# One layout for all dense products: weights held in TensorE, 256 tokens moving, and buffers shifted within 512 bytes

## Chip, cores and metric

The kernel runs on one core of a Trainium2 chip. The metric is the device time of one execution in microseconds, as the median of several runs. Before the change it is 2276.02 us (3 runs, 2275.32 to 2277.13).

## What is computed

A trunk of two layers over one sequence of 256 tokens with 2048 channels, in float32. Layer 0 mixes tokens with a diagonal state-space model (S5), layer 1 with a convolution module; a SwiGLU feed-forward network (FFN) with 5632 hidden channels follows each.

```
for i in range(2):
    shift/scale/gate = split(silu(c) @ ada_w[i] + ada_b[i])        # six vectors of 2048
    h = x * (1 + sc_m) + sh_m
    y = s5(h) then vg = y @ w_glu; vg[:, :d] * sigmoid(vg[:, d:])   # layer 0
    y = glu(h @ w_pw1) -> depthwise conv(31) -> norm -> silu -> @ w_pw2   # layer 1
    x = layer_norm(ALPHA * x + (1 + gt_m) * y)
    h = x * (1 + sc_f) + sh_f
    y = (silu(h @ w_g) * (h @ w_v)) @ w_down
    x = layer_norm(ALPHA * x + (1 + gt_f) * y)
```

The dense products are those with w_glu (2048 x 4096), w_pw1 (2048 x 4096), w_pw2 (2048 x 2048), twice the FFN's gate and value weights (2048 x 11264) and twice w_down (5632 x 2048). Together they read most of the 574 MB that come from HBM; the rest is chiefly ada_w.

## The kernel before

The activations lie with channels on the partitions: X and the input h of a product are tiles of 16 chunks of 128 channels with 256 tokens each. Each float32 product is made of three products in the float32r type: with weights split into whi + wlo and tokens into a high and a low part, it is whi x high, whi x low and wlo x high.

**Units.** A dense product is cut into gemms of 512 output columns, and a gemm into units of four chunks of 128 input channels, 1 MB of weights each. For a unit, SyncE issues the load into one of four raw buffers, ScalarE rounds it to whi (L833) and VectorE takes the remainder as wlo (L834); whi and wlo have two buffers each. Then TensorE runs its matmuls: 4 chunks x 3 products. The pool of these weight buffers is opened in `start_dense`, behind a pool `const2` of small constants; the hidden activations f2 of an FFN lie in pools f0 and f1, opened later. Each pool's start follows from what was allocated ahead of it.

**Two forms.** With `wide` (L889) a 128 x 128 block of the tokens is the operand held in TensorE and 512 columns of weights move past it; a bank of PSUM then holds 128 tokens by 512 output channels. One unit is 24 such matmuls. Without `wide` (L893) a 128 x 128 block of the weights is held and the 256 tokens move; a bank holds two blocks of 128 channels by 256 tokens. One unit is 48 such matmuls. Most gemms are wide. Narrow are the last gemm ahead of each layer norm (last of w_glu, last of w_pw1, first and last of w_pw2, last down gemm of each layer). The first gemm behind each norm but one, `panel` (L1005), also holds the weights; its tokens carry two further columns, 258 in all, so a chunk steps by 1032 bytes.

**After a gemm.** In the wide form the sums have tokens on the partitions, so they are turned: `turned` (L905) makes four 128 x 128 transposes into another PSUM bank. For gated products ScalarE (sigmoid) and VectorE (products) first make the gated tile in SBUF, then that tile is turned. For down and w_pw2 gemms, `add_later` (L1100, L1101) copies both banks to SBUF, one on ScalarE and one on VectorE, and turns the copies. What follows reads the turned bank: `split` (L909, L910: high and low part of the FFN's hidden tile), `residual` (L1060: two multiply-adds on VectorE into X for each of two halves), or `conv_in`, ahead of the convolution.

**What sets the order.** Each engine works its queue in program order. A list called `turning` holds what is put off: `turning.put(n, fn)` runs fn n units later, right after that unit's loads, rounding and remainder have been written down and ahead of its matmuls. All turns are put off by two units. The projection of c (`ada`) is spread over the units as well: a rate says how many of its 1 MB steps go with one unit, a load on SyncE's queue and one multiply-add of 2.1 us on VectorE (L701). PSUM has four accumulator banks; a gemm takes two.

Of the kernel before, what the change touches and what calls it, by code (L numbers as in the profile page):

```python
# [19 lines left out]
P = 128  # L20
# [484 lines left out]
def kernel(  # L505
# [335 lines left out]
    def gemm(wsrc, k0, kch, segs, x2, wp, feed=None, ahead=None, banks=((0, 1), (2, 3)), before={}, acc=None, wide=True):  # L841
# [12 lines left out]
        for u, u0 in enumerate(units):  # L854
# [23 lines left out]
            for part in ((0,), (1,)) if last and not in_turn else ((0, 1),):  # L878
# [5 lines left out]
                for n, (wt, k, h) in enumerate(order):  # L884
                    x = x2(u0 + k)[:, h]
                    first, end = u == 0 and n == 0, last and n == len(order) - 1
                    for bank in part:
                        if wide:
                            nc.tensor.matmul(  # L889
                                acc[bank].rearrange("p a b -> p (a b)"), x[:, bank * HALF:(bank + 1) * HALF], wt[:, k], start=first, stop=end)  # L890
                            continue
                        for i, m in enumerate(banks[bank]):
                            nc.tensor.matmul(  # L893
                                acc[bank][:, i], wt[:, k, m * P:(m + 1) * P], x, start=first and i == 0, stop=end and i == 1)
# [3 lines left out]

    def turned(u, c0, then):

        b = aux("turned")
        for k in range(2):
            for t in range(2):
                o = k * SEQ + t * HALF
                nc.tensor.transpose(b[:, o:o + HALF], u[t][:, c0 + k * P:c0 + (k + 1) * P], ident)  # L905
        then(b.rearrange("p (k n) -> p k n", n=SEQ))
# [168 lines left out]
    def gated(wsrc, off, width, sp, then, entry=None, wide=True, **kw):  # L1075
# [11 lines left out]
        acc = gemm(wsrc, 0, NCH, segs, xh, banks=((0, 2), (1, 3)), wide=wide, **kw)  # L1087
# [4 lines left out]
        if wide:  # L1092
            turning.put(2, lambda: turned([t[:, 0], t[:, 1]], 0, then))
        else:
            then(t)

    def add_later(ys, gt, ch, stats, sp):

        yt = [sp.tile([P, 2, SEQ], F32, tag="sg", name="yt", bufs=2).rearrange("p a b -> p (a b)") for _ in range(2)]
        nc.scalar.copy(out=yt[0], in_=ys[0].rearrange("p a b -> p (a b)"))  # L1100
        nc.vector.tensor_copy(out=yt[1], in_=ys[1].rearrange("p a b -> p (a b)"))  # L1101
        for i in range(2):
            turning.put(2, lambda i=i: turned(yt, 256 * i, lambda b: residual(b, gt, ch + 2 * i, stats)))
# [110 lines left out]
    def ffn(layer, gt, stats, wp, sp, fp, entry, ahead=None, output=None, follow=None):  # L1214

        f0, out = 0, None
        for part, nf in enumerate((24, 20)):
            f2 = fp.tile([P, 24, 2, SEQ], F32R, tag="f2", name=f"f2{layer}{part}")
            fh, fl = f2[:, :, 0], f2[:, :, 1]
            for f in range(0, nf, 2):  # L1220
# [14 lines left out]
                acc = gemm(ffn_w_gu[layer], 0, NCH, gu_cols(f0 + f), xh, wp)  # L1235
# [5 lines left out]
                turning.put(2, lambda t=t, h=fh[:, f:f + 2], l=fl[:, f:f + 2]: turned([t[:, 0], t[:, 1]], 0, lambda b: split(b, h, l)))  # L1241
            ada.finish(layer, 5)
            for q in range(4):
# [6 lines left out]
                ys = gemm(ffn_w_down[layer], f0, nf, [(512 * q, 512)], chunks(f2), wp, ahead=ahead if last else None, wide=not last)  # L1250
# [262 lines left out]
    with mctx:  # L1513
# [19 lines left out]
        for i in range(8):  # L1533
            if i == 7:
                fp = f0ctx.enter_context(tc.tile_pool(name="f0", bufs=1, reuse_waits="tile"))
                raw = entry_raw(fp)
                entry = enter("f0", stats, 0, 0, raw, 7)
            with ExitStack() as order:
                if i == 0:
                    order.enter_context(tc.manual_schedule(engines={mybir.EngineType.PE}))  # L1540
                gated(s5_w_glu[0], 256 * i, D, sp, lambda t, i=i: residual(t, mod[0][:, 2], 2 * i, stats), wp=wp, wide=i < 7,
# [152 lines left out]
        for i in range(8):  # L1694
            ada.hold = i > 5
            gated(cv_w_pw1[0], 256 * i, D, sp, lambda t, i=i: conv_in(i, t), entry if i == 0 else None, wp=wp, wide=i < 7,
# [89 lines left out]
```

## Time and profile before

| | |
|---|---|
| median of the runs | 2276.02 us |
| the profiled execution | 2276.45 us |
| its span, first to last instruction | 2274.7 us |
| mean granted TensorE clock | 0.989 |
| DMA, mean over the span | 255 GB/s |
| S5, before the dense products | 0 to some 200 us |
| w_glu | 200 to 404 us |
| FFN of layer 0 | 404 to 1160 us |
| convolution module | 1160 to 1510 us |
| FFN of layer 1 and the output | 1510 to 2275 us |

The page gives busy time by engine (PE is TensorE's matmuls, PEld its weight loads, DVE VectorE, ACT ScalarE, POOL GpSimd, SP SyncE) and the chain of work that ended last. Groups of instructions are written as "line engine operation output<-inputs". In a timeline a row is a run of like instructions: start in us, us to the end of the last one, and xcount. A matmul's recorded duration runs into its successors, so the price of one in a stream is the distance from one row's start to the next one's, divided by the count.

### The profile page before, as it was taken

How to read it: one execution, taken by the hardware profiler on the slowest of the kernel's cores; microseconds unless marked ns; L12 is line 12 of the kernel's file. 1: busy time of each engine (PE TensorE's matmuls, PEld its weight loads, DVE VectorE, ACT ScalarE, POOL GpSimd, SP SyncE). 2: the span in 40 equal slices, each digit the busy share in tenths (PEclk: the TensorE clock that was granted, in tenths of full speed). 3: DMA queues.
4: the chain of work that ended last, by engine and by line, in shares of the span. 5: the costliest groups of instructions: out<-in, count | busy, mean ns of one | idle time of the engine just before them, and what ended most of it. 6: DMA issues, size and time to landing. Idle time of an engine off the chain costs nothing.

```text
span 2274.7 us, 33445 instructions
## 1 busy us (share of the span) xinstructions
PE 2221.7 (98%) x13619; PEld 1804.2 (79%) x13619; DVE 1671.7 (73%) x1826; ACT 1018.8 (45%) x1237; POOL 157.0 (7%) x265
## 2 busy tenths in 40 slices
PE   7999999999999999999999998999999999999998
PEld 4556778987788888787897786898888888888888
DVE  8897898877777777777988788878755444545474
ACT  4775335644343333343455434556433433434343
POOL 5761000000000000000010110000000000000000
PEclk8999999999999999999999999999999999999998
DMA  9998899599999899999857775757865555555542
GB/s 333 342 317 279 296 340 311 173 313 330 323 328 328 322 321 324 317 327 322 309 157 203 225 213 191 255 191 236 281 222 185 186 195 191 186 185 193 192 165 80
DMA packets 380608, 579.48 MB, mean 255 GB/s; under 512 B 13875, under 2 KB 277939, under 8 KB 365987
## 3 DMA queue, kind: packets, MB, share of 16 engines
q1 hardware_dynamic: 379862, 576.82, 74.9%
q8 instruction: 107, 1.75, 0.3%
q0 software_dynamic: 352, 0.45, 0.1%
q14 instruction: 47, 0.39, 0.1%
q10 hardware_dynamic: 240, 0.08, 0.0%
HBM read 573.72 MB, written 3.57 MB: 254 GB/s over the span
## 4 chain that ended last, share of the span: by engine, by line
PE 79%; DVE 10%; DMA 4%; ACT 4%; issue 2%; SPq 0%; POOL 0%; DVEq 0%; ACTq 0%
PE acc L889 65%; PE acc L893 6%; DVE wlo L834 3%; DMA raw<-in_ffn_w_gu_dram 3%; ACT whi L833 2%; PE acc L1005 2%; PE turned L905 2%; PE conv L1677 1%; DVE adaacc L701 1%; PE y L499 1%; DMA raw<-in_s_w_glu_dram 1%; PE ada L629 1%; DMA raw<-in_ada_w_dram 1%; DVE pin L476 1%; PE adar L709 0%
## 5 line engine op out<-in xcount | busy, mean ns | idle before, releaser
L834 DVE TENSOR_TENSOR wlo<-raw,whi 128x2048 fp32r<-128x2048 f32 x344 | 788.8, 2294 | 456.7 <-ACT whi L833 448.6
L833 ACT CAST whi<-raw 128x2048 fp32r<-128x2048 f32 x344 | 655.6, 1906 | 812.1 <-PE acc L889 442.7
L889 PE MATMUL acc<-whi,h 128*128 128x512 f32 x3648 | 893.4, 394 | 7.6 <-ACT whi L833 7.2
L889 PEld LDWEIGHTS acc<-whi,h 128*128 128x128 f32 x3648 | 680.5, 189 | 161.7 <-ACT whi L833 13.1
L889 PE MATMUL acc<-wlo,h 128*128 128x512 f32 x1824 | 461.8, 390 | 0.8 <-DVE wlo L834 0.6
L889 PEld LDWEIGHTS acc<-wlo,h 128*128 128x128 f32 x1824 | 341.5, 188 | 74.3 <-DVE wlo L834 3.8
L889 PE MATMUL acc<-whi,f 128*128 128x512 f32 x1248 | 300.9, 391 | 0.0
L701 DVE SCALAR_TENSOR_TENSOR adaacc<-rawa,c_act,adaacc 128x2048 f32<-128x2048 f32 (+1 forms) x135 | 284.4, 2107 | 0.4
L889 PEld LDWEIGHTS acc<-whi,f 128*128 128x128 f32 x1248 | 232.8, 188 | 49.5 <-ACT whi L833 1.7
L889 PE MATMUL acc<-wlo,f 128*128 128x512 f32 x624 | 156.5, 389 | 0.0
L889 PEld LDWEIGHTS acc<-wlo,f 128*128 128x128 f32 x624 | 117.1, 188 | 24.3
L1607 POOL TENSOR_TENSOR lw<-fold,wtap 128x1024 f32<-128x1024 f32 x12 | 26.3, 2195 | 1055.5 <-PE acc L893 866.2
L629 PE MATMUL ada<-raw,c_rep 128*32 128x512 f32 (+1 forms) x576 | 71.3, 592 | 6.0 <-DMA raw<-in_ada_w_dram 3.6
L1238 ACT ACTIVATE fsg<-acc 128x256 f32<-128x256 f32 x84 | 31.6, 379 | 97.7 <-PE acc L889 97.7
L893 PEld LDWEIGHTS acc<-h,whi 128*128 128x128 f32 x512 | 63.6, 192 | 8.9 <-ACT h L909 4.2
L893 PE MATMUL acc<-h,whi 128*128 128x256 f32 x512 | 67.3, 286 | 3.4 <-ACT h L909 2.2
L1182 POOL CAST lnmh<-lno 128x2 fp32r<-128x2 f32 x1 | 0.2, 182 | 885.9 <-DVE lno L68 885.9
L1239 DVE TENSOR_TENSOR fsg<-acc,fsg 128x256 f32<-128x256 f32 x84 | 35.0, 418 | 17.0 <-ACT fsg L1238 17.0
L1677 PE MATMUL conv<-vs,lw 128*32 128x256 f32 x720 | 42.2, 380 | 0.1
L893 PE MATMUL acc<-f,whi 128*128 128x256 f32 x320 | 40.7, 284 | 0.0
L893 PEld LDWEIGHTS acc<-f,whi 128*128 128x128 f32 x320 | 39.3, 192 | 0.2
L476 DVE TENSOR_TENSOR_SCAN pin<-rho,pin 128x1024 f32<-128x1024 f32 x16 | 36.7, 2294 | 0.5
(349 smaller groups left out, 1839.7 us busy)
## 6 DMA issues: line engine op xcount, KB each, us to landing
raw<-in_ffn_w_gu_dram SPq DMA_DIRECT2D x352, 512.0 KB, 4.7
rawa<-in_ada_w_dram SPq DMA_DIRECT2D x128, 1024.0 KB, 5.5
raw<-in_ffn_w_down_dram SPq DMA_DIRECT2D x88, 1024.0 KB, 5.1
raw<-in_ada_w_dram SPq DMA_DIRECT2D x64, 1024.0 KB, 7.7
raw<-in_s_w_glu_dram SPq DMA_DIRECT2D x64, 512.0 KB, 5.9
raw<-in_cv_w_pw_dram SPq DMA_DIRECT2D x64, 512.0 KB, 6.0
raw<-in_cv_w_pw_dram SPq DMA_DIRECT2D x16, 1024.0 KB, 5.9
vs<-scr SPq DMA_DIRECT2D x40, 142.0 KB, 5.3
```

The costliest lines, as they stand in the source:

```text
L476: done = v.tensor_tensor_scan(out=z, data0=rh.rearrange("p q r c -> p (q r c)"), data1=z, initial=0.0, op0=MUL, op1=ADD)
L629: nc.tensor.matmul(acc[32 * (k % 4):32 * (k % 4) + 32, :], c_rep[:, kk, :], r[:, k, :], start=kk < 4, stop=kk >= NCH - 4)
L701: nc.vector.scalar_tensor_tensor(out=acc, in0=r[:, i], scalar=c_act[:, kk:kk + 1], in1=acc, op0=MUL, op1=ADD)
L833: m1 = nc.scalar.copy(out=self.hi[:, :kn], in_=r[:, :kn])
L834: m2 = nc.vector.tensor_tensor(out=self.lo[:, :kn], in0=r[:, :kn], in1=self.hi[:, :kn].bitcast(F32), op=SUB)
L889: nc.tensor.matmul(acc[bank].rearrange("p a b -> p (a b)"), x[:, bank * HALF:(bank + 1) * HALF], wt[:, k], start=first, stop=end)
L893: nc.tensor.matmul(acc[bank][:, i], wt[:, k, m * P:(m + 1) * P], x, start=first and i == 0, stop=end and i == 1)
L905: nc.tensor.transpose(b[:, o:o + HALF], u[t][:, c0 + k * P:c0 + (k + 1) * P], ident)
L1005: nc.tensor.matmul(acc[m][:, 0:EW], wt[:, k, m * P:(m + 1) * P], xx[:, 4 * u + k], start=u == 0 and n == 0, stop=u == 3 and n == len(order ...
L1238: nc.scalar.activation(out=t[:, i], in_=gv[:, 0], func=AF.Sigmoid)
L1239: nc.vector.tensor_tensor(out=t[:, i], in0=gv[:, 0], in1=t[:, i], op=MUL)
L1677: nc.tensor.matmul(acc[32 * q:32 * q + 32, :], lw[:, q, g, :], vs[:, q, 4 * g:4 * g + SEQ], start=g == 0, stop=g == n - 1)
```

## The change

- The wide form is gone, and with it `turned` and `add_later`. All gemms hold 128 x 128 blocks of weights and move 256 tokens.
- For the gated products of the FFN each accumulator bank holds one block of gate and the matching block of value channels (`banks=((0, 2), (1, 3))`), as those of w_glu and w_pw1 did in the narrow form.
- What follows a gemm reads the accumulators, or the gated tile in SBUF, directly: the FFN's `split` and the residuals one unit later instead of two, `conv_in` two units later as before.
- Three tiles named "room" are allocated and not used: 48 floats (192 bytes of each partition) ahead of the weight buffers and 80 floats (320 bytes) ahead of f2 in each of the pools f0 and f1. By the change's own words the weight buffers then start at 384, and h and f at 448, modulo 512 bytes. h lies ahead of all of it and doesn't move.

```diff
                     for bank in part:
-                        if wide:
-                            nc.tensor.matmul(
-                                acc[bank].rearrange("p a b -> p (a b)"), x[:, bank * HALF:(bank + 1) * HALF], wt[:, k], start=first, stop=end)
-                            continue
                         for i, m in enumerate(banks[bank]):
                             nc.tensor.matmul(
                                 acc[bank][:, i], wt[:, k, m * P:(m + 1) * P], x, start=first and i == 0, stop=end and i == 1)
...
-    def turned(u, c0, then):
-
-        b = aux("turned")
-        for k in range(2):
-            for t in range(2):
-                o = k * SEQ + t * HALF
-                nc.tensor.transpose(b[:, o:o + HALF], u[t][:, c0 + k * P:c0 + (k + 1) * P], ident)
-        then(b.rearrange("p (k n) -> p k n", n=SEQ))
...
-        if wide:
-            turning.put(2, lambda: turned([t[:, 0], t[:, 1]], 0, then))
+        if wait:
+            turning.put(wait, lambda: then(t))
         else:
             then(t)
-
-    def add_later(ys, gt, ch, stats, sp):
-
-        yt = [sp.tile([P, 2, SEQ], F32, tag="sg", name="yt", bufs=2).rearrange("p a b -> p (a b)") for _ in range(2)]
-        nc.scalar.copy(out=yt[0], in_=ys[0].rearrange("p a b -> p (a b)"))
-        nc.vector.tensor_copy(out=yt[1], in_=ys[1].rearrange("p a b -> p (a b)"))
-        for i in range(2):
-            turning.put(2, lambda i=i: turned(yt, 256 * i, lambda b: residual(b, gt, ch + 2 * i, stats)))
...
-                acc = gemm(ffn_w_gu[layer], 0, NCH, gu_cols(f0 + f), xh, wp)
+                acc = gemm(ffn_w_gu[layer], 0, NCH, gu_cols(f0 + f), xh, wp, banks=((0, 2), (1, 3)))
...
-                turning.put(2, lambda t=t, h=fh[:, f:f + 2], l=fl[:, f:f + 2]: turned([t[:, 0], t[:, 1]], 0, lambda b: split(b, h, l)))
+                turning.put(1, lambda t=t, h=fh[:, f:f + 2], l=fl[:, f:f + 2]: split(t, h, l))
...
-                if not last:
-                    add_later(ys, gt, 4 * q, stats if part == 1 else None, sp)
-                    continue
                 for i in range(2):
+                    if not last:
+                        turning.put(1, lambda y=ys[i], ch=4 * q + 2 * i, s=stats if part == 1 else None: residual(y, gt, ch, s))
+                        continue
...
         const2 = ctx.enter_context(tc.tile_pool(name="const2", bufs=1, reuse_waits="tile"))
+        const2.tile([P, 48], F32, name="room")
...
                 fp = f0ctx.enter_context(tc.tile_pool(name="f0", bufs=1, reuse_waits="tile"))
+                fp.tile([P, 80], F32, name="room")
```

The calls for w_glu (wait of one unit), w_pw1 (wait of two) and w_pw2 (residuals of its second and third gemm one unit later) change in the same way.

More of the change, by code (lines that the diff above doesn't have):

```diff
@@ L839, with gemm @@
     ready, held_back, newest = [], [], None
-    def gemm(wsrc, k0, kch, segs, x2, wp, feed=None, ahead=None, banks=((0, 1), (2, 3)), before={}, acc=None, wide=True):
+    def gemm(wsrc, k0, kch, segs, x2, wp, feed=None, ahead=None, banks=((0, 1), (2, 3)), before={}, acc=None):
         in_turn = acc is not None
@@ L1073, in residual, with gated @@
             stats.add(i, z)
-    def gated(wsrc, off, width, sp, then, entry=None, wide=True, **kw):
+    def gated(wsrc, off, width, sp, then, entry=None, wait=1, **kw):
         segs = [(off, 256), (width + off, 256)]
@@ L1086, in gated @@
             return
-        acc = gemm(wsrc, 0, NCH, segs, xh, banks=((0, 2), (1, 3)), wide=wide, **kw)
+        acc = gemm(wsrc, 0, NCH, segs, xh, banks=((0, 2), (1, 3)), **kw)
         t = sp.tile([P, 2, SEQ], F32, tag="sg", name="sg", bufs=2)
```

17 lines of the change are left out of this document (9 added, 8 removed).

## The prediction, made before the changed kernel ran

> **What bounds the kernel now.** I read the page first (busy shares, the slices, the chain that ended last), then the busy time by stage, then the timeline of single stages.
>
> ```profile
> span 2274.7 us, 33445 instructions
> PE 2221.7 (98%) x13619; PEld 1804.2 (79%) x13619; DVE 1671.7 (73%) x1826; ACT 1018.8 (45%) x1237; POOL 157.0 (7%) x265
> ...
> GB/s 333 342 317 279 296 340 311 173 313 330 323 328 328 322 321 324 317 327 322 309 157 203 225 213 191 255 191 236 281 222 185 186 195 191 186 185 193 192 165 80
> ...
> PE 79%; DVE 10%; DMA 4%; ACT 4%; issue 2%; SPq 0%; POOL 0%; DVEq 0%; ACTq 0%
> ```
>
> TensorE carries 79% of the chain. That is an average, so the stages count. The columns are PE, weight loads, DVE, ACT, POOL, granted clock, DMA share and GB/s:
>
> ```profile
> 200.00:380.00 180.00, 174.58 (x867) 137.54 (x868) 149.62 (x130) 67.34 (x58) 8.78 (x18) 0.97 0.92 313
> ...
> 430.00:680.00 250.00, 248.26 (x1111) 201.91 (x1110) 201.19 (x157) 114.68 (x114) 0.00 (x0) 1.00 0.89 310
> 680.00:848.00 168.00, 167.94 (x770) 137.17 (x769) 128.24 (x85) 61.83 (x41) 0.00 (x0) 1.00 0.91 323
> 848.00:1010.00 162.00, 161.36 (x727) 131.46 (x727) 126.79 (x88) 62.30 (x50) 0.00 (x0) 1.00 0.94 324
> ...
> 1700.00:1960.00 260.00, 260.00 (x1174) 215.65 (x1173) 127.28 (x95) 97.54 (x67) 0.00 (x0) 1.00 0.57 188
> ```
>
> From 430 us on TensorE is never idle for long, at full clock (1.00). In the first FFN the DMA engines are nearly full too (0.91 and 0.94, at 323 and 324 GB/s, where the best slice of the page moved 342); in the second they are not (188). So any change of TensorE's pace goes into the time one for one, except that a gain before 1010 us can run into the DMA.
>
> **What a product costs in either form.** How often each form occurs, before:
>
> ```profile
> L889 PE MATMUL acc<-whi,h 128*128 128x512 f32 x3648 | 893.4, 394 | 7.6 <-ACT whi L833 7.2
> ...
> L889 PE MATMUL acc<-wlo,h 128*128 128x512 f32 x1824 | 461.8, 390 | 0.8 <-DVE wlo L834 0.6
> ...
> L889 PE MATMUL acc<-whi,f 128*128 128x512 f32 x1248 | 300.9, 391 | 0.0
> ...
> L889 PE MATMUL acc<-wlo,f 128*128 128x512 f32 x624 | 156.5, 389 | 0.0
> ```
> ```profile
> L893 PE MATMUL acc<-h,whi x512: 278/283/583, 380.3 to 1508.6; 128*128 128x256 f32 x171
> ...
> L893 PE MATMUL acc<-f,whi x320: 277/283/365, 1130.1 to 2255.6; 128*128 128x256 f32 x160
> ...
> L893 PE MATMUL acc<-h,wlo x256: 279/283/283, 384.2 to 1509.5; 128*128 128x256 f32 x128
> ...
> L893 PE MATMUL acc<-f,wlo x160: 283/283/283, 1133.9 to 2256.5; 128*128 128x256 f32 x160
> ```
>
> That is 3648 + 1824 + 1248 + 624 = 7344 matmuls of 512 columns (tokens held, weights moving) and 512 + 320 + 256 + 160 = 1248 of 256 columns (weights held, tokens moving). Each of the 7344 becomes two of 256. Their mean duration overlaps that of their neighbours, so the price is the distance from start to start. Wide form, in the second FFN:
>
> ```profile
> 1758.97 3.79 PE L889 MATMUL acc<-whi,h 128*128 128x512 f32 x16
> 1762.60 1.98 PE L889 MATMUL acc<-wlo,h 128*128 128x512 f32 x8
> 1764.42 0.60 PE L905 MATMUL turned<-ident,fsg 128*128 128x128 f32 x4
> 1764.77 3.89 PE L889 MATMUL acc<-whi,h 128*128 128x512 f32 x16
> 1768.50 1.98 PE L889 MATMUL acc<-wlo,h 128*128 128x512 f32 x8
> ```
>
> (1762.60 - 1758.97) / 16 = 226.9 ns for 512 columns. Narrow form, in the last panel of the S5 output product:
>
> ```profile
> 390.43 2.08 PE L893 MATMUL acc<-h,wlo 128*128 128x256 f32 x16
> 392.35 4.00 PE L893 MATMUL acc<-h,whi 128*128 128x256 f32 x32
> 396.19 2.08 PE L893 MATMUL acc<-h,wlo 128*128 128x256 f32 x16
> ```
>
> (396.19 - 392.35) / 32 = 120.0 ns for 256, or 240.0 for the pair: 13.1 ns more than the wide form. Two rows give slope and rest: (226.9 - 120.0) / 256 = 0.4176 ns a column, so 256 columns take 106.9 ns, and 13.1 ns is left, once per matmul with its weight load, whatever the length. The change doubles the number of these 13.1 ns. Whether it gains depends on whether they stay.
>
> The load of the next weights goes on while the tokens stream; both read SBUF. In both forms the two buffers lie at the same distance: the change puts 48 floats (192 bytes) ahead of the weight buffers to bring them to 384, so they were at 192, with h at 448, 256 bytes apart modulo 512. f stays at 448, since its own 80 floats fill 192 up to 512. The entry products show other distances, as their tokens step by 1032 bytes from chunk to chunk (258 columns, weights held):
>
> ```profile
> 405.78 2.07 PE L1005 MATMUL acc<-raw,wlo 128*128 128x258 f32 x16
> 407.69 2.07 PE L1005 MATMUL acc<-raw,whi 128*128 128x258 f32 x16
> ...
> 425.52 2.10 PE L1005 MATMUL acc<-raw,wlo 128*128 128x258 f32 x16
> 427.46 2.10 PE L1005 MATMUL acc<-raw,whi 128*128 128x258 f32 x16
> ```
>
> The first group of 16 takes 119.4 ns each, the second 121.3: 107.7 of columns and 11.7 or 13.6 of rest. So the rest moves a little with the addresses, over distances from 256 to 504. After the change h and f lie 64 bytes ahead of the weights, in the half that no row shows. The price is bounded by 106.9 (no rest) and 121.3. The nearest rows by form, the narrow and the entry ones, say 120, and by them nothing is gained. I choose 110 all the same, and it is the weakest step: the rest is the same 13.1 ns under 107 ns of streaming as under 214, so it is no load that is too long to hide but a disturbance between two readers; here the distance is fixed for all 15936 matmuls, so a good one is good for all, where the entry rows change it every four. I put three quarters of the rest as gone.
>
> The Trainium skill speaks against any such effect: "SBUF — State Buffer", section "Who interferes with whom", gives PE two independent read ports, for the moving operand and for LDWEIGHTS, and says that PE never waits on anyone. By it an address does nothing, and the sum is that of the first rival. No row here isolates the ports; the 119.4 beside 121.3 leans against it. For matmuls alone "TensorE: Matmul & The Clock Gate", section "Back-to-back issue gap", gives N/2.4 + 2.5 ns, 109.2 for 256; as an estimate the sum by it would be 115 us less than before, and the rows are 11 ns above it.
>
> **The sum.** Products: 7344 x (2 x 0.1100 - 0.2269) = -50.7 us. The 1248 that were narrow already: x 0.010 = -12.5. The entry products keep their price: 576 matmuls whose distances still vary, 1 ns would be 0.6 us.
>
> The transposes of sums, with what they cost their neighbours:
>
> ```profile
> 719.86 1.03 PE L905 MATMUL turned<-ident,yt 128*128 128x128 f32 x8
> 720.65 3.92 PE L889 MATMUL acc<-whi,f 128*128 128x512 f32 x16
> 724.40 1.98 PE L889 MATMUL acc<-wlo,f 128*128 128x512 f32 x8
> ```
> ```profile
> L905 PE MATMUL turned<-ident,fsg x168: 270/272/331, 460.0 to 2143.5; 128*128 128x128 f32 x168
> ...
> L905 PE MATMUL turned<-ident,yt x128: 270/272/273, 719.9 to 2230.8; 128*128 128x128 f32 x128
> ...
> L905 PE MATMUL turned<-ident,sg x52: 270/272/332, 237.8 to 1357.4; 128*128 128x128 f32 x52
> ```
>
> From the first of four to the end of the next sixteen products 4.08 us pass (1764.42 to 1768.50), against 3.63 without: 0.45. Of eight: 4.54 - 3.63 = 0.91. There are (168 + 52) / 4 = 55 fours and 128 / 8 = 16 eights: 24.8 + 14.6 = -39.3 us, all on TensorE, which is the path.
>
> Evacuation: the copies of the down sums fall away, and the residual reads the accumulators instead of the turned bank, one unit later:
>
> ```profile
> L1100 ACT COPY yt<-acc x16: 587/587/589, 711.9 to 2220.0; 128x512 f32<-128x512 f32 x16
> L1101 DVE COPY yt<-acc x16: 680/691/693, 714.6 to 2222.7; 128x512 f32<-128x512 f32 x16
> ```
>
> ```profile
> L1060 DVE SCALAR_TENSOR_TENSOR X<-turned,mod,X 128x256 f32<-128x256 f32 x78 | 33.2, 476 | 5.1 <-PE turned L905 5.1
> ```
>
> I cost this at nothing. In 16 gemms VectorE loses a copy of 0.69 us and gets the residual's four multiply-adds (4 x 0.476 = 1.9 us) in its place; they wait for the last sum of the gemm before, and behind them on the queue stands the second unit's wlo, for which TensorE waits. That wlo is wanted only after the first unit (5.4 us, 24 x 0.2269) and the second one's 16 matmuls with whi; VectorE is busy for 201 of 250 us in the first window of the first FFN, so there is room. The split of the FFN's gate moves up one unit in the same way. If that cover went, each of these places could cost up to 1.9 us, 30 in all. The accumulators stay taken a unit longer, but there are four of them, and the pair is wanted again only a whole gemm later. No DMA issue is moved past another; SP's queue meets the same units, sooner.
>
> Sum on TensorE: -50.7 - 12.5 - 39.3 = -102.5 us. A dense stage would shorten by 6.9 / 226.9 = 3% and by 0.45 in 22.2, 2%: from 680 to 1010 us the DMA would have to move 323.5 x 1.053 = 341 GB/s, the best slice ever. I take half of that stage's gain (5% of 330 us) as lost: +8. That makes -94.5 on the profiled execution's 2276.45 us (span 2274.7 and 1.75 around it; 0.4 over the median): 2182 us, from 2150 (108.5 ns and no loss to the DMA) to 2212 (111.9 ns).
>
> **The rivals.** Slower: the rest is inherent, or the room doesn't put the buffers where it is meant to, and it stays at 13.1, as 120.0 in every narrow row says. Then 7344 x 0.0131 = +96.2, less 39.3: 2333 us (119.1 to 121.3 ns: 2319 to 2354). It decides from 116.4 ns on, where 15936 matmuls and the old 1816.2 + 39.3 us balance. For it: all narrow rows, and the small swing of the entry rows. Against it: only that this distance was not among them.
>
> The DMA takes the gain: all of the 5% from 200 to 380 and 430 to 1010 us, 38 us, is lost, since the queue is at 0.89 to 0.94 there: -64, 2212 us. Against it: the page has slices of 340 and 342.
>
> The distance helps by little: 116 to 117 ns, as if the best entry group were the best there is; 2276 us.
>
> **How the numbers follow.** Forecast 0.46; slower rival 0.34; DMA 0.09; something between, 112 to 116 ns and 2213 to 2270 us, 0.06; no difference 0.05. Within 0.2% (4.6 us, about what a measurement can tell) there is only a band of 0.6 ns: 0.03. Faster 0.62, slower 0.35. The signs are both likely, so the range must hold both: 2150 to 2340 leaves out some 0.15; the forecast's own is 2150 to 2212.
>
> **What would show it.** After: 20615 matmuls (13619 + 7344 - 348), none on a turned bank; sixteen 256-column matmuls from start to start in 1.76 us in the second FFN. 1.92 there means the first rival. TensorE still without idle time after 1010 us; before, DMA shares near 1.0 and waits of whi for its DMA would mean the DMA rival. Waits of wlo behind the residual would show the evacuation wrongly costed.

## The result, and the profile after

The changed kernel takes 2291.37 us (median of 7 runs, 2283.39 to 2297.15) beside 2276.01 us before (7 runs, 2274.88 to 2277.13): 1.0062 times, 95% interval 1.0043 to 1.0082. It is slower by 0.6%, where 2182 us was forecast. Its profiled execution took 2297.15 us, 20.7 more than the profiled one of before; it is the longest of the seven, so the trace shows 6 us more than the median does.

The page of the changed kernel, the lines that answer to those of before:

```profile
span 2295.2 us, 47413 instructions
PE 2232.5 (97%) x20615; PEld 2116.4 (92%) x20615; DVE 1662.0 (72%) x1810; ACT 1008.2 (44%) x1221; POOL 160.3 (7%) x265
...
GB/s 333 341 321 265 299 351 300 177 317 314 317 328 323 296 301 330 311 311 313 301 194 212 208 223 175 273 196 227 288 220 184 185 196 189 184 184 185 186 181 75
...
PE 70%; DVE 12%; DMA 9%; ACT 5%; issue 3%; SPq 0%; DVEq 0%; ACTq 0%
...
L889 PE MATMUL acc<-h,whi 128*128 128x256 f32 x7808 | 973.2, 280 | 18.7 <-ACT whi L833 14.4
```

20615 matmuls, as forecast. PE is still busy for 97% of the span, but the chain that ended last has 9% DMA where it had 4%, and in front of the commonest group TensorE stood idle for 18.7 us (7.6 before), mostly for whi.

Where the time came from shows when both spans are cut at the same points of the work, the first matmul behind each layer norm. First before, the two FFNs; then after, the two FFNs with the convolution module between them. The columns are the stretch, its length, PE busy, weight loads, DVE, ACT, POOL, granted clock, DMA share, GB/s:

```profile
403.90:1159.70 755.80, 752.48 (x3630) 623.02 (x3629) 597.70 (x464) 318.44 (x284) 0.00 (x0) 1.00 0.88 307
...
1509.70:2274.70 765.00, 758.83 (x3684) 637.89 (x3682) 431.77 (x395) 318.89 (x283) 3.00 (x5) 0.99 0.58 191
```
```profile
405.10:1177.00 771.90, 760.77 (x6443) 750.61 (x6442) 592.20 (x457) 312.88 (x277) 0.00 (x0) 1.00 0.86 301
1177.00:1525.60 348.60, 337.58 (x3281) 306.25 (x3280) 293.63 (x429) 164.28 (x212) 29.20 (x12) 1.00 0.68 212
1525.60:2295.20 769.60, 763.42 (x6496) 760.24 (x6494) 428.69 (x388) 313.86 (x276) 3.01 (x5) 0.99 0.57 190
```

The first FFN grew by 16.1 us, the second by 4.6; the convolution module went from 350.0 (1159.7 to 1509.7, before) to 348.6. In the first FFN half of the growth is idle time of TensorE: 771.90 - 760.77 = 11.1 us where it was 755.80 - 752.48 = 3.3. The other half is busy time. In the second FFN TensorE waits no more than before (6.2 us in both), so the 4.6 us are the price of the products, less the transposes that are gone.

That price, in the second FFN after the change, from start to start:

```profile
1902.47 2.05 PE L889 MATMUL acc<-f,wlo 128*128 128x256 f32 x16
1904.35 3.93 PE L889 MATMUL acc<-f,whi 128*128 128x256 f32 x32
1908.12 2.05 PE L889 MATMUL acc<-f,wlo 128*128 128x256 f32 x16
```

(1908.12 - 1904.35) / 32 = 117.8 ns; sixteen take 1.88 us, where the forecast wanted 1.76 and the slower rival 1.92. But not everywhere. In the first FFN, still after the change (the bracket is idle time before a row and what ended it):

```profile
479.58 3.79 PE L889 MATMUL acc<-h,whi 128*128 128x256 f32 x32
483.21 1.98 PE L889 MATMUL acc<-h,wlo 128*128 128x256 f32 x16
486.14 4.04 PE L889 MATMUL acc<-h,whi 128*128 128x256 f32 x32 [0.96 <-ACT whi L833]
490.02 2.05 PE L889 MATMUL acc<-h,wlo 128*128 128x256 f32 x16
```

(483.21 - 479.58) / 32 = 113.4 ns up to here; then comes a wait of 0.96 us, and behind it (490.02 - 486.14) / 32 = 121 with the restart in it, and then 117.8 until 562 us, over four further interruptions and on the same buffers. So one layout has two lasting rhythms: intervals of 113, 113, 114 ns, or of 117, 118, 118. Each holds until an interruption (a wait, the projection's own matmuls, an entry product) and can be another one behind it; in the traces of the change and of runs 4, 6, 8, 10 and 11 below no stream changes its rhythm without one. Counted over the whole trace, 2048 of the 15936 matmuls with 256 columns run in the short rhythm, the others in the long one: 117.2 ns on average. The forecast rested on 110, and its own turning point was 116.4.

With 117.2 put into the prediction's formula: 15936 x 0.1172 - 1816.2 - 39.3 = +12.2 us. The additional idle time of the first FFN, 7.8 us, brings it to 20.0 of the 20.7 that were measured.

### The profile page after: what moved, and what is told of

The parts are those of the page before. It is cut to its first block, busy times and chain, and to the rows that moved or that the text cites. A ratio compares the mean times of both kernels' runs of the same rounds, so it can differ in the third digit from the quotient of the medians.

```text
span 2295.2 us, 47413 instructions
## 1 busy us (share of the span) xinstructions
PE 2232.5 (97%) x20615; PEld 2116.4 (92%) x20615; DVE 1662.0 (72%) x1810; ACT 1008.2 (44%) x1221; POOL 160.3 (7%) x265
## 4 chain that ended last, share of the span: by engine, by line
PE 70%; DVE 12%; DMA 9%; ACT 5%; issue 3%; SPq 0%; DVEq 0%; ACTq 0%
PE acc L889 63%; DMA raw<-in_ffn_w_gu_dram 5%; DVE wlo L834 4%; ACT whi L833 3%; DMA raw<-in_ffn_w_down_dram 2%; PE conv L1658 2%; DVE adaacc L701 1%; DMA raw<-in_s_w_glu_dram 1%; PE acc L992 1%; PE y L499 1%; DVE pin L476 1%; PE adar L709 0%; PE ada L629 0%; DMA raw<-in_ada_w_dram 0%; PE out L1141 0%
## 5 line engine op out<-in xcount | busy, mean ns | idle before, releaser
L889 PE MATMUL acc<-h,whi 128*128 128x256 f32 x7808 | 973.2, 280 | 18.7 <-ACT whi L833 14.4
L889 PEld LDWEIGHTS acc<-h,whi 128*128 128x128 f32 x7808 | 938.5, 188 | 37.8 <-ACT whi L833 19.0
L889 PE MATMUL acc<-h,wlo 128*128 128x256 f32 x3904 | 507.6, 279 | 1.3 <-DVE wlo L834 1.1
L889 PEld LDWEIGHTS acc<-h,wlo 128*128 128x128 f32 x3904 | 478.4, 188 | 3.1 <-DVE wlo L834 2.9
L889 PE MATMUL acc<-f,whi 128*128 128x256 f32 x2816 | 349.8, 280 | 2.4 <-ACT whi L833 2.4
L889 PEld LDWEIGHTS acc<-f,whi 128*128 128x128 f32 x2816 | 338.9, 188 | 4.9 <-ACT whi L833 3.9
L889 PE MATMUL acc<-f,wlo 128*128 128x256 f32 x1408 | 183.1, 280 | 0.7 <-DVE wlo L834 0.7
L889 PEld LDWEIGHTS acc<-f,wlo 128*128 128x128 f32 x1408 | 173.0, 188 | 1.5 <-DVE wlo L834 1.4
L1047 DVE SCALAR_TENSOR_TENSOR X<-acc,mod,X 128x256 f32<-128x256 f32 x80 | 34.4, 478 | 25.0 <-PE acc L889 25.0
L1218 DVE TENSOR_TENSOR fsg<-acc,fsg 128x256 f32<-128x256 f32 x84 | 35.1, 420 | 17.1 <-ACT fsg L1217 17.1
L1219 DVE TENSOR_TENSOR fsg<-acc,fsg 128x256 f32<-128x256 f32 x84 | 35.3, 422 | 1.9
```

Source lines behind the costliest of these rows:

```text
L889: nc.tensor.matmul(acc[bank][:, i], wt[:, k, m * P:(m + 1) * P], x, start=first and i == 0, stop=end and i == 1)
L1047: nc.vector.scalar_tensor_tensor(out=X[:, ch + k], in0=y[:, k], scalar=gt[:, ch + k:ch + k + 1], in1=X[:, ch + k], op0=MUL, op1=ADD)
L1218: nc.vector.tensor_tensor(out=t[:, i], in0=gv[:, 0], in1=t[:, i], op=MUL)
L1219: nc.vector.tensor_tensor(out=t[:, i], in0=gv[:, 1], in1=t[:, i], op=MUL)
```

## The experiments

The theory after the result, called A: the price depends on where weights and tokens lie relative to each other, the new layout wins only a little of the 13.1 ns, and the rest of the loss is loads in the first FFN that come too late. Its rival B: the place does nothing, the lower price comes from something else in the rewritten program, and the waits come from the earlier evacuation. In what follows "distance" is the tokens' start less the weights' start, modulo 256 bytes: 0 before, 64 after. "Waits within the products" are what the intervals from start to start over 130 ns (260 for 512 columns) hold above the usual one, restarts included.

**1. The change without its rooms.** The weights go back to 192, distance 0.

```diff
-        const2.tile([P, 48], F32, name="room")
...
-                fp.tile([P, 80], F32, name="room")
```

> The changed kernel without its three rooms: weights held everywhere, weight buffers back at 192, h and f at 448 modulo 512. Theory A (the place of the buffers sets the price of a matmul with its weight load): every stream of 256-column matmuls runs at 120.0 ns, as the narrow gemms did before, never at 113 or 118; 15936 x (120.0 - 117.1) = 46 us more than the changed kernel, some 2337 us. Rival (the places do nothing, the price fell because all gemms have one form now): 117 to 118 ns and some 2291 us.

2319.18 us (2318.22 to 2322.32), 1.0194 [1.0179, 1.0209]. The second FFN of this kernel:

```profile
1903.21 4.00 PE L889 MATMUL acc<-f,whi 128*128 128x256 f32 x32
1907.05 2.08 PE L889 MATMUL acc<-f,wlo 128*128 128x256 f32 x16
```

(1907.05 - 1903.21) / 32 = 120.0 ns, and 119.9 to 120.0 as the mean of each stage. Program and order are those of the change; only addresses differ, and the price goes from 117.2 to 120.0. B falls. The second FFN takes 787.9 us, 22.9 more than before, which is the slower rival's arithmetic for that stage (2952 x 13.1 ns less 140 transposes: 38.7 - 15.8 = 22.9). The whole stayed below the expectation because of the first FFN: 771.7 us, the same as with the rooms. Its products take 737.1 us where the change's take 720.2, but its waits within the products are 1.6 us against 18.7. What the better place saved there went into waiting.

**2. The kernel before with the rooms alone.** Wide form, distance 64.

```diff
+        const2.tile([P, 48], F32, name="room")
...
+                fp.tile([P, 80], F32, name="room")
```

> The kernel before, with the rooms alone: tokens held as before, weight buffers at 384. Theory A: the wide matmul's rest of 13.1 ns falls as the narrow one's did, to 6.4 or 10.9, so 220 to 225 ns instead of 226.9; over 7344 matmuls 16 to 49 us less than before, 2227 to 2260 us. Rival (only a held weight block feels the place): 226.9 ns and 2276 us.

2308.37 us (2305.09 to 2308.92), 1.0141 [1.0126, 1.0157]: slower, where A had it faster. The second FFN:

```profile
1902.83 3.89 PE L889 MATMUL acc<-whi,f 128*128 128x512 f32 x16
1906.56 2.03 PE L889 MATMUL acc<-wlo,f 128*128 128x512 f32 x8
```

(1906.56 - 1902.83) / 16 = 233.1 ns instead of 226.9. The narrow gemms of the same kernel run at 117.8. The place counts for both forms, but they want different places, which A had not allowed for: the layout that helps 256 columns by 2 ns costs 512 columns 6.

**3. A map of places.** Not the trunk: bursts of 48 matmuls on one pair of buffers, in the narrow and in the wide form, for 8 x 8 starts in steps of 64 bytes.

```diff
+    def burst(name, wo, xo, wide):
+        wt = wb[:, 16 * wo:16 * wo + 2048].rearrange("p (k n) -> p k n", k=4)
+        xt = xb[:, 16 * xo:16 * xo + 2048].rearrange("p (k a n) -> p k a n", k=4, a=2)
...
+                if wide:
+                    nc.tensor.matmul(acc[b], xt[:, k, h, 128 * b:128 * b + 128], wt[:, k], start=n == 0, stop=end)
+                    continue
...
+                    nc.tensor.matmul(acc[b][:, 256 * i:256 * i + 256], wt[:, k, 128 * m:128 * m + 128], xt[:, k, h], start=n == 0 and i == 0, stop=end and i == 1)
```

> A bench, no trunk is computed (x is copied to the output): bursts of 48 matmuls, weights in one buffer and tokens in another, each moved in steps of 64 bytes over 512, 64 pairs of places; for each pair four bursts with weights held and 256 tokens moving, and one with tokens held and 512 weights moving. Each burst begins after a wait of TensorE for ScalarE. Theory A: the price of a matmul depends on the places, 120.0 at (192, 448), 113.3 or 117.8 at (384, 448), other values elsewhere. Rival: 118 to 120 at all 64 pairs. If the four bursts of one pair differ, the start decides too.

The mean interval over the last 24 matmuls of each burst, worked out from the trace (w: 512 columns, n: 256):

```
distance      0      64     128     192
n         120.0   117.8   118.7   113.3
w         226.7   233.3   232.5   228.9
```

Only the distance counts; all places of one distance agree within 1.5 ns, but for four bursts at distance 192 with the weights at 128 or 384, which ran at 117.8 (the table has the price of the other 60). Distances of 256 and more repeat the first four. In the timeline of this kernel (a: start 0, c: 128, d: 192, e: 256, f: 320; the weights' letter comes first):

```profile
117.08 11.67 PE L44 MATMUL wac<-wb,xb 128*128 128x512 f32 x48 [0.50 <-ACT res L50]
129.26 6.00 PE L48 MATMUL nad<-xb,wb 128*128 128x256 f32 x48 [0.50 <-ACT res L50]
135.76 6.00 PE L48 MATMUL nad<-xb,wb 128*128 128x256 f32 x48 [0.50 <-ACT res L50]
...
167.28 6.26 PE L48 MATMUL nae<-xb,wb 128*128 128x256 f32 x48 [0.50 <-ACT res L50]
174.04 6.26 PE L48 MATMUL nae<-xb,wb 128*128 128x256 f32 x48 [0.49 <-ACT res L50]
...
206.24 6.17 PE L48 MATMUL naf<-xb,wb 128*128 128x256 f32 x48 [0.50 <-ACT res L50]
212.91 6.18 PE L48 MATMUL naf<-xb,wb 128*128 128x256 f32 x48 [0.50 <-ACT res L50]
```

From burst to burst 6.50 us at distance 192 (nad), 6.76 at 0 (nae), 6.67 at 64 (naf). The bursts begin slower, so the settled prices lie a little further apart than 0.26 / 48. The best of the map is 113.3, 3.1 ns under the turning point and still 6.4 over the 106.9 that the prediction took for the columns.

**4. The change with the evacuation two units later, as it was before.**

```diff
-                turning.put(1, lambda t=t, h=fh[:, f:f + 2], l=fl[:, f:f + 2]: split(t, h, l))
+                turning.put(2, lambda t=t, h=fh[:, f:f + 2], l=fl[:, f:f + 2]: split(t, h, l))
...
-                        turning.put(1, lambda y=ys[i], ch=4 * q + 2 * i, s=stats if part == 1 else None: residual(y, gt, ch, s))
+                        turning.put(2, lambda y=ys[i], ch=4 * q + 2 * i, s=stats if part == 1 else None: residual(y, gt, ch, s))
```

> The changed kernel with what follows a gemm two units later instead of one (the split of the gate, the residuals, the product with w_glu). Theory A: the evacuation costs nothing and it stays at some 2291 us, within the spread of the runs. Rival (the residual ahead of wlo makes the 8 us of new waits in the first FFN): 2283 us, with waits there back to some 11 us.

2284.34 us (2282.51 to 2288.52), 1.0040 [1.0026, 1.0055]. The products cost the same (117.2 ns), the first FFN is 764.5 us with 12.1 us of waits in place of 18.7. These are nearly the rival's numbers, 2283 us and 11 us of waits. The time is 7 us under the change's median, but at the lower end of the spread of its runs (2283 to 2297), and other waits mean other rhythms, so this run doesn't decide. Run 8 repeats it on another layout.

**5. The map in steps of 8 bytes,** the same bursts, weights at one place, distances 0 to 248; the edit is against run 3.

```diff
-        xt = xb[:, 16 * xo:16 * xo + 2048].rearrange("p (k a n) -> p k a n", k=4, a=2)
+        xt = xb[:, xo:xo + 2048].rearrange("p (k a n) -> p k a n", k=4, a=2)
...
-            for xo in range(8):
+        for j in range(32):
...
+                burst("n" + name, 0, 2 * j, False)
+            burst("w" + name, 0, 2 * j, True)
```

> The bench again (no trunk is computed, x is copied to the output), weights at 0 and tokens at 32 places 8 bytes apart from 0 to 248. The coarse map showed the price to depend on the distance from weights to tokens modulo 256 alone: 120 at 0, 118 at 64, 119 at 128, 113.3 at 192. Theory A (a phase between two readers): between these the price moves in small steps, and 113.3 is met over some stretch around 192; a still lower one, toward 106.9, may lie between. Rival (lines of 64 bytes): four flat levels, or worse prices off the multiples of 64.

No narrow place goes below 113.3. At 112 all four bursts have it; at 64 one of four, and at 192 too only one of four, where the map of run 3 had it in nearly every burst. All other places lie between 116.7 and 121.5, but for two of the four bursts at 104, which run at 130. The price does not move in small steps from place to place, as the expectation had it. The wide form has its 226.7 at 0, 120 and 240 and is otherwise mostly at 231 to 233.

**6. The change with the weights at 256,** distance 192, the best of the first map.

```diff
-        const2.tile([P, 48], F32, name="room")
+        const2.tile([P, 16], F32, name="room")
...
-                fp.tile([P, 80], F32, name="room")
+                fp.tile([P, 112], F32, name="room")
```

> The changed kernel with the weight buffers at 256 instead of 384 (room of 16 floats), h and f still at 448: a distance of 192. Theory A: every stream runs at 113.3 from start to end; the products of both FFNs fall from 1439 to 1393 us, those of the S5 output and the convolution by 7 and 9, so 60 us less than the changed kernel where TensorE is the bound, 2232 us; with half of the first FFN's gain lost to waits for loads 2244. Rival (the bench's price doesn't hold in the kernel, streams fall into a slow rhythm after a wait): 117 to 118 and some 2290 us.

2275.94 us (2267.4 to 2283.7), 1.0009 [0.9994, 1.0023]: a tie with the kernel before, and the expectation missed. In the profiled execution 8729 of the 15936 matmuls run in the short rhythm. The second FFN loses it early:

```profile
1649.42 3.79 PE L889 MATMUL acc<-h,whi 128*128 128x256 f32 x32
1653.05 1.98 PE L889 MATMUL acc<-h,wlo 128*128 128x256 f32 x16
1654.96 1.05 PE L709 MATMUL adar<-adaacc,ones 128*32 128x512 f32 x4
1655.94 3.92 PE L889 MATMUL acc<-h,whi 128*128 128x256 f32 x32
1659.69 1.98 PE L889 MATMUL acc<-h,wlo 128*128 128x256 f32 x16
1661.60 0.46 PE L717 MATMUL adat<-ident,adas 64*128 64x64 f32 x4
1661.98 2.15 PE L889 MATMUL acc<-h,whi 128*128 128x256 f32 x16
1663.97 1.10 PE L889 MATMUL acc<-h,wlo 128*128 128x256 f32 x8
1664.91 0.28 PE L889 MATMUL acc<-h,whi 128*128 128x256 f32 x1
```

113.4 ns ahead of the projection's four matmuls (L709). Behind them the short rhythm goes on: (1659.69 - 1655.94) / 32 = 117.2 has the restart in it, whose first interval alone takes 222 ns, and the sixteen with wlo take 1.98 us again. It is lost at the next interruption, the four of L717: (1664.91 - 1663.97) / 8 = 117.5, and 117.8 for some 500 us after that, in which nothing interrupts the stream. So distance 192 has both rhythms in the kernel, as 64 has, with a better mixture. In the first FFN the price is 114.4 ns, but the waits within the products rise to 23.5 us.

**7. The same, without 73 loads of the projection in the first FFN.** Each step there reads the tile h in place of its 1 MB from HBM.

```diff
+            if self.rate == 0.77 and layer == 1 and n == 2048:
+                r = h_all[:, 0:2048].bitcast(F32).rearrange("p (k n) -> p k n", n=n)
+                return lambda: self.add(layer, j, b0, k, r)
```

> The kernel with the weight buffers at 256, and in the first FFN the 73 steps of layer 1's projection of c read a tile that is there already instead of loading 1 MB each; the projection is then not the reference's. Theory B (the waits of the first FFN are for HBM): its waits of TensorE for whi, 19 us in the changed kernel's profile, fall under 3 us, and the stage takes some 730 us (6144 x 0.1133 and 33 of other work). Rival (they come from VectorE's or ScalarE's queue): the waits stay.

2257.92 us (a single execution; this kernel leaves out loads, so its projection is not the reference's). The first FFN of run 6, then of this run:

```profile
404.40:1163.80 759.40, 745.02 (x6442) 733.89 (x6441) 592.18 (x456) 312.96 (x277) 0.00 (x0) 1.00 0.87 306
```
```profile
399.40:1140.30 740.90, 737.73 (x6442) 731.22 (x6442) 593.46 (x457) 314.79 (x277) 0.00 (x0) 1.00 0.64 211
```

With the same work on all engines and a third less to load (211 GB/s in place of 306), TensorE's idle time falls from 14.4 us to 3.2, the waits within the products from 23.5 to 6.0, and the stage by 18.5, if not to the 730 us expected. The waits of the first FFN are for loads; no instruction on VectorE or ScalarE was taken away. But a step without a load doesn't take one of the four raw buffers either, so this run doesn't tell whether the loads are late because the memory gives no more or because they are issued late.

**8. Run 6 with the evacuation two units later** (the edit of run 4 on it).

```diff
-                turning.put(1, lambda t=t, h=fh[:, f:f + 2], l=fl[:, f:f + 2]: split(t, h, l))
+                turning.put(2, lambda t=t, h=fh[:, f:f + 2], l=fl[:, f:f + 2]: split(t, h, l))
...
```

> The kernel with the weight buffers at 256, and what follows a gemm two units later instead of one. With one steady price the time of the evacuation shows by itself: Theory A says equal to the one-unit form within 3 us, the rival (residual and split ahead of the second unit's wlo and whi make waits) says 5 to 8 us less.

2276.06 us (2266.39 to 2280.36), 0.9999 [0.9987, 1.0012]; run 6 has 1.0009. No difference. In the first FFN there are fewer waits (14.2 against 23.5 us) and dearer products (115.7 against 114.4 ns), 757.9 us against 759.4. At this layout it is worth nothing that can be measured when the evacuation comes.

**9. Which start gives which rhythm.** Bursts of 96 matmuls at 16 distances, with twelve starts each: one without a filler and eleven behind fillers of matmuls of different lengths.

```diff
+        if filler:
+            t = psum.tile([P, 512], F32, tag="fill", name="fill", bufs=2)
+            nc.tensor.matmul(t[:, 0:32], raw[:, 0:P], raw[:, 0:32], start=True, stop=True)
+            nc.tensor.matmul(t[:, 32:32 + filler], raw[:, 0:P], raw[:, 0:filler], start=True, stop=True)
```

> A bench (no trunk is computed, x is copied to the output): weights held, 256 tokens moving, 16 distances from 0 to 240 bytes in steps of 16, and for each of them 12 bursts of 96 matmuls whose starts differ: one directly after a wait for ScalarE, eleven behind two filler matmuls, the second of a different length each time. The fine map showed two prices at distances 64 and 192 (117.8 and 113.3), one alone, 113.3, at 112. Theory C (two rhythms between the stream and the load of the next weights; the start picks one, the distance says which exist): at 64 and 192 both occur over the starts and each holds to the end of its burst, at 112 all twelve run at 113.3, at 0 all at 120.0. Rival (the start decides everything, the distance little): about the same mixture at every distance, 112 too.

The groups of this kernel at distances 0 (faa), 64 (fae), 112 (fah) and 192 (fbe), eleven bursts each; the first number behind the bar is the busy time, tails included:

```profile
L49 PE MATMUL faa<-xb,wb 128*128 128x256 f32 x1056 | 132.3, 285 | 0.4
...
L49 PE MATMUL fae<-xb,wb 128*128 128x256 f32 x1056 | 130.2, 282 | 0.5
...
L49 PE MATMUL fah<-xb,wb 128*128 128x256 f32 x1056 | 126.0, 278 | 0.5
L49 PE MATMUL fbe<-xb,wb 128*128 128x256 f32 x1056 | 125.8, 278 | 0.5
```

Settled, 112 and 192 have 113.3 ns in all twelve bursts, 64 has 117.8 in all, and 0 has 120.0. Half of the expectation missed: no filler turned 64 or 192 into the other rhythm. So what picks the rhythm at 64 and 192 isn't the length of the filler alone, and stays open. What holds in both finer maps is 112.

**10. The change at distance 112:** weights at 352, h and f read from 464, four floats further into their tiles.

```diff
-        const2.tile([P, 48], F32, name="room")
+        const2.tile([P, 40], F32, name="room")
...
-    h2 = h_all[:, 0:2 * NCH * SEQ].rearrange("p (k a t) -> p k a t", a=2, t=SEQ)
+    h2 = h_all[:, 4:4 + 2 * NCH * SEQ].rearrange("p (k a t) -> p k a t", a=2, t=SEQ)
...
-            f2 = fp.tile([P, 24, 2, SEQ], F32R, tag="f2", name=f"f2{layer}{part}")
+            f2 = fp.tile([P, 48 * SEQ + 8], F32R, tag="f2", name=f"f2{layer}{part}")[:, 4:4 + 48 * SEQ].rearrange("p (k a t) -> p k a t", a=2, t=SEQ)
...
-                fp.tile([P, 80], F32, name="room")
+                fp.tile([P, 88], F32, name="room")
```

> The changed kernel with the weight buffers at 352 and h and f read from 464, modulo 512: a distance of 112, at which every start of the bench ran at 113.3. Theory C: every stream of the kernel runs at 113.3; against the kernel with the weights at 256 the second FFN's products fall from 716 to 696 us, those of the S5 output and the convolution by 6, and what the first FFN gains goes mostly into its waits for loads: 2276 - 26 = 2250 us (2243 to 2256). Rival (in the kernel each wait throws the stream into either rhythm at any distance): a mixture again, 114.5 to 117, and some 2276 us.

2257.97 us (2252.97 to 2261.23), 0.9928 [0.9916, 0.9940]: faster than before. In its second FFN:

```profile
1901.11 3.79 PE L889 MATMUL acc<-f,whi 128*128 128x256 f32 x32
1904.74 1.98 PE L889 MATMUL acc<-f,wlo 128*128 128x256 f32 x16
```

113.4 ns, and the short rhythm for 6079 of 6144 products of that stage. The stage is 744.6 us, 20.4 less than before. The first FFN of the same kernel gives nothing:

```profile
405.90:1169.20 763.30, 744.58 (x6442) 731.82 (x6441) 592.09 (x456) 313.53 (x277) 0.00 (x0) 1.00 0.87 305
```

It is 763.3 us, 7.5 more than before, with 18.7 us of idle TensorE and waits within the products of 31.8 us; the products cost 113.7. That is why the whole lies over the expectation.

**11. Run 10 with loads of the projection moved out of the first FFN** into the convolution module.

```diff
-        ada.rate, ada.behind = 0.77, True
+        ada.rate, ada.behind = 0.68, True
...
-        ada.rate = 0.25
+        ada.rate = 0.4
```

> The same with fewer of the projection's 1 MB steps in the first FFN (0.68 a unit instead of 0.77) and more in the convolution (0.4 instead of 0.25). Theory B (the first FFN's waits are for HBM): some 11 MB less there, at 330 GB/s up to 33 us of transfer, bring 5 to 12 us of the waits back; the convolution has room: 2238 to 2245 us. Rival (VectorE, at 82% in the convolution, passes it on): no gain, or 5 us more than without.

2237.42 us (2236.28 to 2245.91), 0.9842 [0.9829, 0.9856], the fastest version here. Its first FFN and convolution module:

```profile
405.40:1136.20 730.80, 729.85 (x6430) 725.09 (x6429) 571.80 (x445) 313.94 (x276) 0.00 (x0) 1.00 0.86 304
1136.20:1498.40 362.20, 339.64 (x3293) 303.35 (x3292) 316.83 (x441) 165.07 (x213) 29.19 (x12) 0.97 0.73 233
```

TensorE's idle time in the first FFN falls from 18.7 us to 0.95, the waits within the products from 31.8 to 2.5 and the stage by 32.5, far more than the 5 to 12 us expected, at nearly the same rate (304 GB/s) with less to load; the convolution module gives 16.7 of it back (345.5 to 362.2). The profiled execution is the longest of its five, so its stages stand some 8 us over the median.

**12. The kernel before with the same shift of loads.**

```diff
-        ada.rate, ada.behind = 0.77, True
+        ada.rate, ada.behind = 0.68, True
...
-        ada.rate = 0.25
+        ada.rate = 0.4
```

> The kernel before with the same shift of the projection's steps (0.68 a unit in the first FFN, 0.4 in the convolution), and nothing else: tokens held, weights at 192. Theory B (loads hold TensorE up only where it runs faster than they come): in the form before, the waits of the first FFN are 11 us and those of the convolution grow by some 12, so 2270 to 2280 us. Rival (the shift is a gain of its own, whatever the form): 15 to 20 us less, 2256 us.

2283.77 us (2281.86 to 2284.74), 1.0041 [1.0027, 1.0054]: slower. That is over the 2270 to 2280 expected, since the convolution module lost 20 us and not 12 (350.0 to 370.2). The first FFN falls only from 755.9 to 748.9 us; TensorE was busy for all but 3.3 us of it before. Of the two kernels the shift pays in run 11, where the products outrun the loads, and not here.

## Why the prediction was wrong, and where it was right

**The step that failed is the 110 ns,** "I put three quarters of the rest as gone". At the new layout 2.8 of 13.1 ns are gone on average (117.2), less than a quarter; 7.2 ns more for each of 15936 matmuls are 115 us, the whole way from the forecast to the profiled execution. The argument for it was half right: it is an effect of how two operands lie to each other (runs 1 to 3), and a fixed distance does serve all matmuls. But from this it didn't follow that the distance chosen by the change is a good one. Of four distances in steps of 64 bytes it is the second best, and the very best in any map leaves 6.4 ns. The other half fails: "the rest is the same 13.1 ns under 107 ns of streaming as under 214" was put in and not found, since two rows give just two unknowns. At the other distances of run 3 the same sum gives 2 x 117.8 - 233.3 = 2.3 ns at 64 and 2 x 113.3 - 228.9 = -2.3 at 192. So there is no common rest of which a share could go, and 106.9 ns for the columns is a figure of distance 0 alone. The range of the forecast itself, 2150 to 2212, wanted 108.5 to 111.9 ns, which no place of the maps showed. The rule of the Trainium skill ("TensorE: Matmul & The Clock Gate", section "Back-to-back issue gap") that gives 109.2 ns for 256 columns, and that the section states for an isolated matmul's gap, isn't reached by these streams, which load new weights for each matmul; 113.3 is their lowest.

**The rival that came nearest** is the one with 0.05, "the distance helps by little": 116 to 117 ns and 2276 us. Its mechanism is what the runs show; its time is 15 us short, for the price of 117.2 and for the waits. The entry products, 119.4 and 121.3, said it: they were rows at other distances, and they moved by 2 ns. They are at 119.8 to 120.0 on average in every kernel here, the fastest too. The prediction dismissed them because their distance changes every four matmuls; that reason stands, but a row that can't show a gain is no evidence for one.

**"By it an address does nothing"**: the independent read ports that the Trainium skill states ("SBUF — State Buffer", section "Who interferes with whom") would make run 1 equal to the change. It is 28 us slower, from three unused tiles alone, and the map has 113.3 to 120.0 ns for the same instructions. The measurement decides: the place counts. That it is the read ports which collide is argued, not shown; no run looks inside.

**The slower rival's arithmetic is right** where its condition holds: run 1 has 120.0 ns in each dense product and +22.9 us in the second FFN. As a whole it gives 2319 instead of 2333. Half of the difference lies in the first FFN, which grew by 15.8 us and not 22.9: before, TensorE had 3.3 us of idle time there and its products had waits of 10.9 us, and dearer products left 0.4 and 1.6. The rest lies in the stages of w_glu and the convolution, and its cause stays open. The turning point of 116.4 holds in the second FFN, where little is waited for: 117.0 ns in the change is 4.6 us over before, 116.6 in run 6 is 0.6 over, 113.4 in run 10 is 20.4 under. For the whole kernel it lies lower, because of the first FFN: run 6, with 115.3 on average, is only a tie.

**The transposes and the count**: in the second FFN, 670.1 + 28.8 + 12.9 + 3.1 us (wide, narrow, transposes, waits between them) became 718.9 + 0.8. So the products rose by 20.0, and transposes and waits fell by 15.2; the prediction's prices give 21 x 0.45 + 7 x 0.91 = 15.8 for the 21 fours and 7 eights of that stage. The 20615 matmuls came out exactly.

**Evacuation at nothing** is borne out by runs 6 and 8 (1.0009 and 0.9999); at the change's own layout run 4 leaves up to 7 us open. TensorE's products wait 1.9 us in all for wlo after the change.

**The DMA.** The prediction took half of a 5% gain from 680 to 1010 us as lost, 8 us, because the best slices moved 342 GB/s. But a stage lives on its mean: over the whole first FFN no kernel with all its loads moved more than 307 GB/s, and the kernel before is one that did. No version with all its loads in place took less time there than before: 755.8 us before, 763.3 with the price at its best (run 10), 771.9 with the change. Of before, of the change and of run 10 the row of TensorE's waits for whi ahead of the products, over the span (us, times, longest):

```profile
PE acc L889 <- ACT whi L833: 7.2, 6, 3.1
```
```profile
PE acc L889 <- ACT whi L833: 16.8, 17, 3.1
```
```profile
PE acc L889 <- ACT whi L833: 24.4, 23, 3.1
```

The cheaper the products, the more often TensorE meets a whi that isn't there; run 7 shows that the load is behind it. That 307 GB/s is all the memory gives isn't shown. Ahead of the wait that ends at 486.14 us in the first FFN's rows further up, the change moved 370 GB/s from 474 to 480 us and 186 from 480 to 484, and SyncE issued no load between these two rows:

```profile
474.64 0.92 SPq L585 DMA_DIRECT2D raw<-in_ffn_w_gu_dram  x2
481.71 0.34 SPq L686 DMA_DIRECT2D rawa<-in_ada_w_dram  x1
```

So the number of raw buffers, and VectorE, which frees them, are a rival to the memory that no run separates. Why the change's own execution moved 301 GB/s there and run 4's 305, with the same loads, is open. The DMA rival, with its 38 us lost, had it right that the loads take the gain, at a price of products that never came. That the 8 us taken for it and the 7.8 us of additional idle time are alike is luck: the 8 were half of a gain, and there was no gain. Its sign came by half: there are waits for whi, but the DMA share of the stage is 0.86 and not near 1.0.

**The spread.** The changed kernel's runs differ by 14 us, those of before beside them by 2. Two rhythms, chosen anew behind each wait, could do this: 15936 x 4.5 ns = 72 us lie between all long and all short. But only one execution of each kernel has a trace, and beside runs 6 to 8 the kernel before too went from 2268 to 2283 us; the cause of the spread stays open.

## What to carry to other kernels

Before a stream of matmuls with a weight load each is rewritten, work out the price at which the new form breaks even (here 116.4 ns), and measure start to start on a few dozen products at several distances of the two operands, in steps of 16 bytes and behind several starts; a place is chosen by that, not by the hope that another is better. A layout that is good for one form can be bad for the other. And before a gain of TensorE is counted in a stage full of loads, look at the mean GB/s over that whole stage and not at its best slice: here the gain became waiting until loads were moved elsewhere (run 11).

## What the runs showed of the hardware that was not expected

- In float32r, with new weights for each matmul, the price depends on the distance of the two operands modulo 256 bytes: in steps of 64 bytes 113.3 to 120.0 ns for 256 columns, 226.7 to 233.3 ns for 512 (best at 0). The two forms have opposite preferences at 0. Between these steps 112 bytes has 113.3 ns in every burst, and 104, 8 bytes beside it, 120 or 130.
- At one distance there can be two lasting rhythms, 113.3 and 117.8 ns, on the same buffers at full clock. Distance 112 showed the short one nearly throughout (6079 of 6144 products in run 10), 64 and 192 both. What picks it is open.
